# Sums of output-projection weights placed at other stages, weight loads on another queue, and two block products interleaved by token tile

## The chip, the cores and the metric

The program runs on one core of one Trainium2 chip. The core has five engines, which work at the same time and meet through semaphores: TensorE (PE: matrix products and transposes), VectorE (DVE), ScalarE (ACT), GpSimd (POOL) and SyncE (SP), which here only issues transfers. ACT and POOL can issue transfers too. Each engine, and each engine's line of transfers, works its instructions off in order. The metric is the device time of one execution in microseconds (us), lower being better.

## The reference, cut to what matters

The model is a trunk of two decoder layers over 1024 positions of width 1024, everything in float32. Layer 0 has latent attention, layer 1 sliding-window attention; in both, four cross-attention heads over 256 memory rows run beside them, and all heads go through one output projection `w_o`, followed by a squared-ReLU MLP.

```python
for i in range(DEPTH):
    hn = rmsnorm(x, attn_norm_g[i])
    mix, q_cross = mla_mixer(...) if i % 2 == 0 else swa_mixer(...)
    cross = memory_cross_attention(q_cross, mem_n, w_mem_kv[i])
    x = x + jnp.concatenate([mix, cross], axis=-1) @ w_o[i]
    x = x + squared_relu_mlp(rmsnorm(x, mlp_norm_g[i]), mlp_w_up[i], mlp_w_down[i])
return rmsnorm(x, final_norm_g)
```

## The kernel before

**Precision.** PE multiplies in a reduced float32 form, so every operand is split into a high and a low part (`split`, L94: ACT copies the high part, L99; DVE subtracts to get the low part, L100), and a product takes three PE instructions (high x high, high x low, low x high).

**Order.** The source gives a program order. When the kernel is built, a planner simulates the engines with its own costs and fixes each engine's order: an instruction goes when its inputs are ready, earlier program order first. So an instruction can stand on its engine well ahead of its place in the source, and on the chip the fixed order is kept even if another instruction would be ready. A tile whose memory overlaps an older tile waits until that one has been used for the last time.

**The output projection** is a Strassen-like scheme with seven block products (`wo_phase`, from L1203): the 1024 x 1024 product is cut in halves by token, by feature and by column, and `steps` lists the products in the order 1, 5, 6, 3, 2, 7, 4, four steps (k-tiles) each, 28 in all. Each step is 12 PE instructions: four token tiles j, three products each. `prep` splits the activation block of a step and loads its weights, `mm(n, j)` does step n for token tile j, `add(p, j)` adds the finished bank to the running result, `stat` stores it and forms half a sum of squares, `norm(t)` finishes the norm of tile t, `xT_(t)` transposes the normed tile for the MLP. Products 6, 7 and 4 accumulate in the same four PSUM banks Y as product 1. Steps 20 to 23 are product 7, steps 24 to 27 product 4. Before, steps 0 to 23 each run all four token tiles; product 4 then runs tile by tile. Tiles 0 to 3 are finished by product 2, tiles 4 to 7 by products 7 and 4.

**The weight sums** that this scheme needs are made beforehand by `wo_sums`. For each of 8 units (n = 0 to 7; k-tile n // 2, column quarter n % 2) it loads four blocks of 128 x 256 of `w_o` (L585, or L590 for layer 1, where a block is two half loads), makes four DVE subtractions (L619 to L622), splits each of the four results (high part to a buffer of `his`, low part in place) and stores both parts to scratch memory `wt`, eight stores of 128 KB a unit (L611), all on SP's line. It is a generator: the code around it calls `next(summing)` where a piece is to go. `sets` are the load buffers, `his` the buffers of the high parts; a buffer is used again only when its store is done.

- Layer 0: one set and four `his`, in spare quarters of the tile f1. Two `next` calls stand ahead of each of the nine later turns of the loop over token tiles in the input projection (L667 to L681): one unit a tile. A turn transposes tile k (`a_T`), projects tile k - 1 (`a_in`) and transposes the compressed tile k - 2 (`a_cT`). After it come the values (`values_of`) together with cross-attention (`cross`: score products, a maximum on DVE, exponentials on ACT, a scaling on POOL, transposes, value products), and then the keys and queries of the heads, with head buffers in the pool `hb`.
- Layer 1: two sets of four quarters of f1 and three `his` (the tile wos in the pool wosp). The projection runs ten jobs (L2073: values, keys, then six of queries, numbers 4 to 9), each of two token halves with 24 products (`feat_mm`, L109 to L111). `in_w` (L1942) loads one job's raw weights (512 KB, L1947, one of two buffers "raw"), POOL scales them (L1951) and `split` makes wf, one of two pairs. The load of job n + 1 is asked for at the start of job n. From job 4 on, two `next` calls stand ahead of each half. A positions tile, posb, takes one of the two raw buffers at job 4, and POOL makes the eight distance tiles from it (L2024 to L2028). The queries q1 are twelve tiles of 128 x 1024; q1[10] and q1[11] are written by job 9.

## Time and profile before

| what | us |
|---|---|
| median of three runs | 2142.35 (2137.09 to 2142.85) |
| profiled execution, timed | 2142.25 |
| its span, first to last instruction | 2140.5 |
| mean granted clock of PE | 0.994 |
| input projection of layer 0, first to last product | 47.5 to 144.6 |
| output projection of layer 0, products 7 and 4 | 509.1 to 535.9 |
| query jobs 4 to 9 of layer 1, first to last product | 1263.2 to 1350.3 |
| output projection of layer 1, start of product 7 | 1474.8 |

How to read the rows quoted below. In a timeline: start in us, duration, engine, line of the source, operation, written tile <- read tiles, shapes, count of merged instructions, and in brackets the idle time before it with what ended it. In a table of waits: who waited, for whom, us in total, times, longest. In a table of windows: the stretch, its length, then for PE, PE's weight loads, DVE, ACT and POOL the busy us and the instructions, then PE's granted clock, the mean busy share of the 16 transfer engines, and GB/s. In a table of lines: line, engine, operation, tiles, shapes and count, then busy us, mean ns of one, and the idle time before them with what ended it. A PE instruction's duration overlaps the next one's, so the pace is read from start to start. "SPq" is SP's line of transfers.

### The profile page before, as it was taken

Reading aid. Unit: us, or ns where it says so; the run is one execution under the profiler, and the core shown is the slowest. Engines: PE = TensorE matmul, PEld = TensorE weight load, DVE = VectorE, ACT = ScalarE, POOL = GpSimd, SP = SyncE. Lnnn points to the kernel's source line nnn. Section 1 sums busy time; section 2 is a strip of 40 time slices with the busy share of each in tenths; the row PEclk is TensorE's granted clock in tenths of the full one; section 3 lists DMA queues with packets and bytes.
Section 4 is the critical chain, followed back from the end, with each engine's and each line's share of the span. In section 5 each row is a group of like instructions: output and inputs, shape, how many; then the busy total and the mean of one; then the engine's idle time right before and its main releaser. Section 6 shows DMA issues by size and latency. Waiting matters only on the chain. (4 is left out here: it accounts for less than half of the span.)

```text
span 2140.5 us, 29718 instructions
## 1 busy us (share of the span) xinstructions
PE 2070.5 (97%) x9832; PEld 1690.8 (79%) x9832; DVE 1543.8 (72%) x3011; ACT 1150.0 (54%) x2504; POOL 161.9 (8%) x224
## 2 busy tenths in 40 slices
PE   7999999999899999999999997999999999999998
PEld 6888778777687878888888876778778778888886
DVE  7675688876976776976557466897987766976565
ACT  5555477767654444444445553877654443444452
POOL 0013100001000000000011331531000000000000
PEclk9999999999999999999999998999999999999999
DMA  8532225266244446944432236147254446955342
GB/s 270 175 102 71 49 63 131 55 202 211 94 157 162 149 140 227 322 147 152 142 119 90 66 93 192 41 132 247 89 168 162 138 133 220 327 162 154 117 119 89
DMA packets 209796, 314.43 MB, mean 147 GB/s; under 512 B 21629, under 2 KB 101994, under 8 KB 209642
## 3 DMA queue, kind: packets, MB, share of 16 engines
q1 hardware_dynamic: 203200, 296.77, 43.6%
q0 software_dynamic: 4016, 13.12, 1.7%
q10 hardware_dynamic: 2426, 2.65, 0.4%
q8 instruction: 77, 1.26, 0.3%
q14 instruction: 77, 0.63, 0.1%
HBM read 206.34 MB, written 93.63 MB: 140 GB/s over the span
## 5 line engine op out<-in xcount | busy, mean ns | idle before, releaser
L1403 ACT ACTIVATE mr<-mr,gcol 128x256 f32<-128x256 f32 (+1 forms) x160 | 67.8, 478 | 80.2 <-DMA mr<-in_mlp_w_up_dram 73.0
L1403 ACT ACTIVATE d<-d,gcol 128x256 f32<-128x256 f32 x128 | 57.5, 500 | 89.1 <-DMA d<-in_mlp_w_up_dram 81.6
L1844 PE MATMUL psy<-g 128*128 128x512 f32 x256 | 99.9, 390 | 0.0
L1845 PE MATMUL psy<-g 128*128 128x512 f32 x256 | 99.6, 389 | 0.0
L1846 PE MATMUL psy<-g 128*128 128x512 f32 x256 | 99.3, 389 | 0.0
L99 ACT ACTIVATE g<-i 128x512 fp32r<-128x512 f32 x79 | 49.6, 628 | 87.8 <-PE psz L1845 45.0
L100 DVE TENSOR_TENSOR g<-i,g 128x512 fp32r<-128x512 f32 x79 | 55.5, 702 | 48.5 <-ACT g L99 48.3
L99 ACT ACTIVATE uh<-i 128x512 fp32r<-128x512 f32 x66 | 41.6, 630 | 86.3 <-PE psy L1845 40.7
L99 ACT ACTIVATE i<-mr 128x512 fp32r<-128x512 f32 x78 | 49.0, 628 | 71.1 <-PE psy L1845 20.7
L953 ACT ACTIVATE p<-pss 128x512 f32<-128x512 f32 x108 | 63.6, 593 | 42.5 <-PE pss L932 42.3
L100 DVE TENSOR_TENSOR pl<-p,ph 128x512 fp32r<-128x512 f32 (+1 forms) x96 | 61.7, 652 | 25.4 <-ACT ph L99 24.8
L807 DVE TENSOR_REDUCE m<-psx 128x1 f32<-128x128 f32 (+5 forms) x96 | 70.3, 749 | 11.3 <-PE psx L803 11.2
L100 DVE TENSOR_TENSOR uh<-i,uh 128x512 fp32r<-128x512 f32 x66 | 45.6, 690 | 45.1 <-ACT uh L99 44.8
L1844 PE MATMUL psz<-g 128*128 128x512 f32 x192 | 74.7, 389 | 0.0
L1845 PE MATMUL psz<-g 128*128 128x512 f32 x192 | 74.7, 389 | 0.0
L1846 PE MATMUL psz<-g 128*128 128x512 f32 x192 | 74.7, 389 | 0.0
L100 DVE TENSOR_TENSOR i<-mr,i 128x512 fp32r<-128x512 f32 x78 | 53.7, 688 | 22.5 <-ACT i L99 22.2
L1725 DVE TENSOR_TENSOR mqf<-mqq,mqf 128x512 f32<-128x512 f32 x64 | 43.1, 687 | 22.5 <-DMA mqq<-in_mlp_w_down_dram 22.3
L99 ACT ACTIVATE ph<-p 128x512 fp32r<-128x512 f32 (+1 forms) x96 | 56.4, 599 | 1.3
L1845 PEld LDWEIGHTS psy<-g 128*128 128x128 f32 x256 | 48.1, 188 | 9.9
L1846 PEld LDWEIGHTS psy<-g 128*128 128x128 f32 x256 | 48.0, 188 | 10.0
L1507 PE MATMUL psu<-g,i 128*128 128x512 f32 x120 | 49.3, 411 | 6.8 <-ACT d L1546 4.1
(703 smaller groups left out, 6975.9 us busy)
## 6 DMA issues: line engine op xcount, KB each, us to landing
i<-hd SPq DMA_DIRECT2D x154, 256.0 KB
hd<-uh SPq DMA_DIRECT2D x76, 256.0 KB
hd<-ul SPq DMA_DIRECT2D x76, 256.0 KB
mr<-in_mlp_w_up_dram SPq DMA_DIRECT2D x36, 512.0 KB
hd<-x SPq DMA_DIRECT2D x72, 256.0 KB
mr<-hd SPq DMA_DIRECT2D x70, 256.0 KB
d<-in_mlp_w_up_dram SPq DMA_DIRECT2D x32, 512.0 KB
mqq<-in_mlp_w_down_dram SPq DMA_DIRECT2D x32, 512.0 KB
```

Source lines behind the costliest of these rows:

```text
L99: r = nc.scalar.activation(hi, src, AF.Copy)
L100: nc.vector.tensor_tensor(lo, src, f32(hi), ALU.subtract)
L807: nc.vector.reduce_max(m8s[h][:, i : i + 1], ps[:, c], axis=AX, negate=True)
L953: nc.scalar.activation(p, ps, AF.Exp, scale=SC)
L1403: nc.scalar.activation(w[:, k, :], w[:, k, :], AF.Copy, scale=g_mlp[layer][:, k0 + k : k0 + k + 1])
L1507: nc.tensor.matmul(ps, wh[:, k, :], xh[:, k, :], start=p in (1, 2, 5) and k == 0, stop=False, skip_group_check=True)
L1725: G(self.b(a, k), self.b(c, k), self.b(a, k), SUB)
L1844: nc.tensor.matmul(ps, ah[:, j, :], bh, start=p in (1, 5, 2) and k == 0, stop=False, skip_group_check=True)
L1845: nc.tensor.matmul(ps, ah[:, j, :], bl, start=False, stop=False, skip_group_check=True)
L1846: nc.tensor.matmul(ps, al[:, j, :], bh, start=False, stop=k == NP - 1, skip_group_check=True)
```

## The change

It has four edits.

1. Layer 0's sums are cut in two. Units 0 to 3 stay in the input projection with one set, at half the pace: one `next` ahead of the transposes and one behind the projection, and with one set the generator has extra empty steps, so that a unit takes two tiles, with a step between load and subtractions and one between subtractions and splits. Units 4 to 7 go to the values loop, two `next` calls behind each of tiles 2 to 7, with four sets and eight `his` in a new tile of 24 KB a partition (pool wop). All four are loaded as soon as the tile may be written. The pool is released ahead of `hb`, whose buffers take its memory.
2. Layer 1's `his` become eight quarters of q1[10] and q1[11]; the pool wosp goes.
3. The raw weights of jobs 4 to 9 are loaded from ACT's line and not from SP's.
4. In `wo_phase`, in both layers, the preparations of steps 24 to 27 and the norms of tiles 0 to 3 stand ahead of step 20. Products 7 and 4 then run tile by tile in the order 7.0, 7.1, 4.0, 7.2, 4.1, 7.3, 4.2, 4.3, each with its add, stat and (for 4) norm; `xT_` 0 to 5 follow the second to sixth and the last of these.

```diff
-    def wo_sums(layer, sets, his):
+    def wo_sums(layer, ns, sets, his):
...
-        V, ct, ns = nc.vector.tensor_tensor, [0], len(sets)
+        V, ct, step = nc.vector.tensor_tensor, [0], len(sets)
...
         def run():
-            for n in range(ns):
+            for n in ns[:step]:
                 load(n)
             yield
-            for n in range(8):
+            if step == 1:
+                yield
+            for n in ns:
...
                 V(s[3], s[3], s[2], ALU.subtract)
+                if step == 1:
+                    yield
                 put(n, 0)
                 put(n, 1)
                 yield
                 put(n, 2)
                 put(n, 3)
-                if n + ns < 8:
-                    load(n + ns)
+                if n + step in ns:
+                    load(n + step)
                 yield
+                if step == 1:
+                    yield
...
-    summing = wo_sums(0, [quarters[0:4]], quarters[4:8])
+    summing = wo_sums(0, range(4), [quarters[0:4]], quarters[4:8])
...
-        for _ in range(2 if k else 0):
+        if k:
             next(summing, None)
...
             a_in(k - 1)
+        if k:
+            next(summing, None)
...
+    wop = pool("wop")
+    wos = wop.tile([P, 24, 256], F32, name="wos")
+    wos = [wos[:, i, :] for i in range(24)]
+    summing = wo_sums(0, range(4, 8), [wos[i : i + 4] for i in range(0, 16, 4)], wos[16:])
+    next(summing)
...
         values_of(t)
+        for _ in range(2 if t > 1 else 0):
+            next(summing, None)
...
+    wop.release()
     hb = pool("hb")
...
-        for n in range(N - 4):
+        for n in range(N - 8):
...
+        for n in range(nprep, N):
+            prep(n)
+        for i in range(2):
+            q = m.quad(f"q{i}", F32R)
+            X[i + 1] = [q[:, 0:4, :], q[:, 4:8, :]]
         for j in range(4):
-            for n in range(N - 4, N):
+            norm(j)
+        for i, (p, j) in enumerate(((7, 0), (7, 1), (4, 0), (7, 2), (4, 1), (7, 3), (4, 2), (4, 3))):
+            for n in range(20 if p == 7 else 24, 24 if p == 7 else 28):
                 mm(n, j)
-            add(4, j)
-            stat(4 + j, 0)
-            norm(4 + j)
-            if j:
-                xT_(2 + j)
+            add(p, j)
+            stat(4 + j, int(p == 7))
+            if p == 4:
+                norm(4 + j)
+            t = {1: 0, 2: 1, 3: 2, 4: 3, 5: 4, 7: 5}.get(i)
+            if t is not None:
+                xT_(t)
...
-            nc.sync.dma_start(out=raw, in_=wsv[:, :, c0 : c0 + P])
+            (nc.scalar if wf is not None else nc.sync).dma_start(out=raw, in_=wsv[:, :, c0 : c0 + P])
...
-                wosp = pool("wosp")
-                wos = wosp.tile([P, 3, 256], F32, name="wos")
-                summing = wo_sums(1, [quarters[0:4], quarters[4:8]], [wos[:, e, :] for e in range(3)])
+                wos = [f32(q1[10 + i_ // 4][:, (i_ % 4) * 256 : (i_ % 4) * 256 + 256]) for i_ in range(8)]
+                summing = wo_sums(1, range(8), [quarters[0:4], quarters[4:8]], wos)
...
-    wosp.release()
```

More of the change, by code (lines that the diff above doesn't have):

```diff
@@ L590, in w_rows @@
             nc.sync.dma_start(out=dst[g * 64 : g * 64 + 64], in_=w_o[layer, h * 64 : h * 64 + 64, cols])
-    wts = {}
-    def wo_sums(layer, sets, his):
-        ds = wts[layer] = {p: [dram.tile([P, 4, 512], F32, name=f"wt{layer}_{p}{e}") for e in "hl"] for p in (5, 7, 6, 4)}
-        V, ct, ns = nc.vector.tensor_tensor, [0], len(sets)
+    wts = [{p: [dram.tile([P, 4, 512], F32, name=f"wt{layer}_{p}{e}") for e in "hl"] for p in (5, 7, 6, 4)} for layer in range(2)]
+    def wo_sums(layer, ns, sets, his):
+        V, ct, step = nc.vector.tensor_tensor, [0], len(sets)
         def load(n):
@@ L601, in load @@
             for i, (kt, e) in enumerate(((k, 0), (k, 1), (k + 4, 1), (k + 4, 0))):
-                w_rows(layer, kt, slice(e * 512 + c * 256, e * 512 + c * 256 + 256), sets[n % ns][i])
+                w_rows(layer, kt, slice(e * 512 + c * 256, e * 512 + c * 256 + 256), sets[n % step][i])
         def put(n, i):
             k, c = divmod(n, 2)
-            s = sets[n % ns][i]
+            s = sets[n % step][i]
             hi, lo = his[ct[0] % len(his)].bitcast(F32R), s.bitcast(F32R)
@@ L609, in put @@
             split(s, hi, lo)
-            for d_, t_ in zip(ds[(5, 7, 6, 4)[i]], (hi, lo)):
+            for d_, t_ in zip(wts[layer][(5, 7, 6, 4)[i]], (hi, lo)):
                 nc.sync.dma_start(out=d_[:, k, c * 256 : c * 256 + 256], in_=f32(t_))
         def run():
-            for n in range(ns):
+            for n in ns[:step]:
                 load(n)
             yield
-            for n in range(8):
-                s = sets[n % ns]
+            if step == 1:
+                yield
+            for n in ns:
+                s = sets[n % step]
                 V(s[0], s[1], s[0], ALU.subtract)
@@ L1367, in wo_phase @@
                 m.fill.append(fills[n // 14]())
-            if n == 20:
-                for i in range(2):
-                    q = m.quad(f"q{i}", F32R)
-                    X[i + 1] = [q[:, 0:4, :], q[:, 4:8, :]]
             for j in range(4):
```

7 lines of the change are left out of this document (removed).

## The prediction

> **What bounds the kernel now.** I read the page first, then PE's waits and windows in each of the stages that the diff touches, and last the timelines of the engines there.
>
> ```profile
> PE 2070.5 (97%) x9832; PEld 1690.8 (79%) x9832; DVE 1543.8 (72%) x3011; ACT 1150.0 (54%) x2504; POOL 161.9 (8%) x224
> PEclk9999999999999999999999998999999999999999
> ```
>
> PE is busy for 97% of the span, so time is to be had only where PE stands still or runs slowly. One slice of the 40 has a lower granted clock, about 1284 to 1337 us. That is layer 1's query projection, where the second edit lies. PE's waits from 1263 to 1352 have one row, and the windows show the stretch and the one before it:
>
> ```profile
> PE psf L109 <- ACT wf L99: 13.8, 3, 6.9
> core 0: us, PE busy (x) PEld busy (x) DVE busy (x) ACT busy (x) POOL busy (x), PEclk, DMA share, GB/s
> 1263.00:1290.00 27.00, 27.00 (x121) 22.36 (x120) 18.22 (x33) 12.28 (x25) 12.14 (x30) 1.00 0.48 152
> 1290.00:1340.00 50.00, 36.16 (x153) 29.23 (x152) 31.25 (x68) 20.80 (x50) 7.95 (x9) 0.86 0.59 182
> ```
>
> All of PE's 13.8 us of waiting is for split weights (wf), three times. The timelines of POOL, ACT, PE and SP say why:
>
> ```profile
> 1274.89 0.49 POOL L2028 TENSOR_SCALAR_AFFINE_SELECT df<-df 128x128 f32<-128x128 f32 x1
> 1277.66 1.22 DVE L100 TENSOR_TENSOR wf<-wsr,wf 128x1024 fp32r<-128x1024 f32 x1
> 1294.72 0.40 SPq L611 DMA_DIRECT2D wt_7l<-fb  x1
> 1295.23 0.38 SPq L1947 DMA_DIRECT2D wsr<-in_swa_w_in_dram  x1
> 1299.91 1.90 POOL L1951 TENSOR_TENSOR wsr<-wsr,gcol 128x1024 f32<-128x1024 f32 x1 [24.53 <-DMA wsr<-in_swa_w_in_dram]
> 1301.84 1.06 ACT L99 ACTIVATE wf<-wsr 128x1024 fp32r<-128x1024 f32 x1 [1.19 <-POOL wsr L1951]
> 1302.95 0.80 PE L109 MATMUL psf<-xnh,wf 128*128 128x512 f32 x1 [6.92 <-ACT wf L99]
> 1313.60 0.42 SPq L1947 DMA_DIRECT2D wsr<-in_swa_w_in_dram  x1
> 1327.76 0.39 SPq L1947 DMA_DIRECT2D wsr<-in_swa_w_in_dram  x1
> ```
>
> Job 7's raw weights go into the buffer of posb, which POOL has finished with when its last distance tile ends at 1275.4; they are issued at 1295.2, after stores of the weight sums (L611) on the same queue. So the load stands some 20 us behind other traffic in SP's line; POOL idles 24.5 us for it, ACT follows, PE comes last. Job 8's buffer is free at 1278.9, when DVE's split of job 6 ends, and its load is issued at 1313.6.
>
> What holds SP is seen in the waits of SP and of ACT:
>
> ```profile
> SPq L611 <- ACT wos L99: 21.1, 7, 16.3
> ACT wos L99 <- DMA wt_6h<-wos: 6.7, 5, 2.2
> ACT wos L99 <- DMA wt_5h<-wos: 6.6, 3, 3.8
> 1253.08 0.42 DVE L406 COPY fb<-psco 128x256 f32<-128x256 f32 x1
> 1263.00 0.39 PE L111 MATMUL psf<-xnh,wsl 128*128 128x512 f32 x1
> 1264.64 1.03 ACT L99 ACTIVATE wos<-fb 128x256 fp32r<-128x256 f32 x3
> ```
>
> SP waits 16.3 us in one piece for the first split of a sum. That split starts right after job 3's last product, since the three buffers wos lie where job 3's split weights lay. (The row at 1253.08 is the last of the cross-attention, for later.) Afterwards the splits wait 13.3 us for a store to give one of the three buffers back.
>
> **The change, part by part.**
>
> *Layer 1's loads and sums.* The loads of jobs 4 to 9 go from SP's line to ACT's; the sums' high parts go to eight quarters of q1[10] and q1[11]. One job is 48 products:
>
> ```profile
> 1263.23 0.39 PE L109 MATMUL psf<-xnh,wf 128*128 128x512 f32 x1
> 1274.11 0.39 PE L109 MATMUL psf<-xnh,wf 128*128 128x512 f32 x1
> 1350.05 0.39 PE L111 MATMUL psf<-xnh,wf 128*128 128x512 f32 x1
> ```
>
> 10.88 us a job, 0.227 us a product. Six jobs need 65.3 us; they take 87.0 (1263.2 to 1350.3). Of the 21.7 between, 13.8 are the waits. Part of the rest is score products that stand there in both kernels, part is slow clock: 1290 to 1340 lacks at most 14% of 50 us, 7 us, some of it while PE idled anyway; I take 3.5. So the edit can give 0 to 17.3 us.
>
> What is late next? From issue to DVE's split the chain is 4.7 (1295.23 to 1299.91), then 1.9, 1.06 and 1.22, some 9 us, less than a job. Job 7's load, issued by 1276, is split by 1286 and needed at 1296; job 8's is split when job 6 gives its wf buffer back at 1296 and needed at 1307; job 9's likewise 11 us later. The load adds a wait to ACT, whose line is in order: behind it stand the evictions of q, and behind those PE, which has four banks, 5.44 us each. The wait must therefore outlast some 16 us to be felt. Six issues at 0.4 us are hidden in ACT's idle (29.2 of 50 us).
>
> The sums stay slow. Of the eight rows of stores, the first and the last by time:
>
> ```profile
> L611 SPq DMA_DIRECT2D wt_5h<-wos x8: 344/382/535, 1265.1 to 1325.8; - x8
> L611 SPq DMA_DIRECT2D wt_4l<-fb x8: 319/400/448, 1270.0 to 1331.9; - x8
> ```
>
> Eight units in 67 us, 8.4 us each, since a unit's loads follow the stores of the unit two before. But they start earlier. q1 lies over the cross-attention's buffers and job 2's split weights, free at about 1253 (its last eviction) rather than 1263. Eleven us of start, and fewer waits for buffers, put the last store from 1332 to about 1318 (my estimate). Job 9's evictions into q1[10] and q1[11], the new wait, come at about 1323. Yet ACT's and DVE's orders are fixed at build time, and a split of wf behind a late sum is late with it; for that I leave 2.3 us. **15 us less**, ends 0 and 17.3, nearest to the waits' row.
>
> *Layer 0's sums.* Lines of 100 to 146 by shape, waits of PE from 48 to 146, and the windows:
>
> ```profile
> L619 DVE TENSOR_TENSOR fa<-fa 128x256 f32<-128x256 f32 x4 | 1.7, 426 | 10.7 <-DMA fa<-in_w_o_dram 10.7
> L100 DVE TENSOR_TENSOR fa<-fa 128x256 fp32r<-128x256 f32 x16 | 6.0, 419 | 0.0
> PE psct L573 <- DVE qc L340: 1.6, 2, 1.0
> PE psct L574 <- POOL fa L304: 1.4, 2, 0.9
> PE psT_a L208 <- DVE xhls L100: 1.3, 3, 0.7
> 146.00:190.00 44.00, 41.78 (x293) 36.22 (x294) 29.06 (x62) 30.45 (x103) 17.39 (x12) 1.00 0.08 21
> ```
>
> In four units DVE stands 10.7 us for w_o, and PE loses 4.3 us to DVE's lateness (rope's POOL included). With a unit every second tile and a step between load and subtraction most of this goes: 3 us less, ends 0 and 4.3. The other four units go to the values stage: 8 DVE instructions each at 0.42 make 13.4 us, against 14.9 us of DVE idle in 146 to 190; 16 ACT splits (three took 1.03 us above) make 5.5 against 13.5. DMA share there is 0.08, so SP's 16 loads and 32 stores find a free line, but they can start only when the input weights' memory is free. In sum it fits, in order it will not quite: behind a subtraction stand softmax maxima, behind those PE. I take 2.5 us more, ends 0 and 13.4 (nothing hidden). Head 0's buffers now wait for the last of these stores; no product of this stage reads them, so I take nothing for it. **0.5 us less.**
>
> *The last two block products.* The instructions are the same ones in another order. DVE's adds, SP's last load of product 4's operands and PE's first use of them, and the windows of each layer:
>
> ```profile
> L1291 DVE TENSOR_TENSOR d<-pswy,d 128x512 f32<-128x512 f32 x4 | 2.7, 686 | 0.4 <-PE pswy L1287 0.3
> 1471.53 0.32 SPq L1261 DMA_DIRECT2D mqf<-wt_4l  x1
> 1488.83 0.48 PE L1285 MATMUL pswy<-mqf,g 128*128 128x512 f32 x1
> 500.00:530.00 30.00, 29.86 (x145) 24.20 (x145) 18.48 (x50) 22.81 (x56) 5.17 (x11) 1.00 0.51 185
> 530.00:570.00 40.00, 35.66 (x169) 27.69 (x167) 38.97 (x79) 31.10 (x66) 1.44 (x3) 1.00 0.13 47
> 1460.00:1495.00 35.00, 34.64 (x168) 28.58 (x167) 21.14 (x51) 27.76 (x67) 7.08 (x13) 1.00 0.69 245
> 1495.00:1535.00 40.00, 36.21 (x163) 28.21 (x163) 38.84 (x81) 30.18 (x65) 1.62 (x3) 0.96 0.13 46
> ```
>
> After the products DVE is full (39.0 and 38.8 of 40 us) and PE loses 4.3 and 3.8 us; before it DVE has 11.5 and 13.9 us free. A tile's product is 12 x 0.227 = 2.7 us. Tile 4's last product becomes third of eight instead of fifth, 5.4 us sooner; tile 5's fifth instead of sixth, 2.7 us sooner; tiles 6 and 7 stay. So one or two tiles' work (four DVE subtractions at 0.69 and a norm) may move into the free time, if ACT, also near full, brings their transposes. New waits: product 4 of a tile now waits for add 7 in the same bank, 0.69 us under the 2.7 of the product between; and its operands, the last issued at 1471.5 and first used at 1488.8, are needed 5.4 us sooner, with 11.9 to spare. I take 1.5 us a layer, **3 us less**, ends 8.1 less (all of both losses) and 4 more (an add late behind DVE's line in every second turn).
>
> *Sum.* The profiled execution took 2142.25 us, span 2140.5 and 1.75 around it; the three runs have the median 2142.35, so no correction. 2142.25 - 15 - 0.5 - 3 = 2123.75: **2124 us**.
>
> A page of the Trainium skill speaks against the first term: "DMA: Bandwidth & Descriptors", section "Issuing engines are not separate DMA queues", has it that issuing from several engines saves only the sequencer's time to start a transfer, usually small beside the transfer.
>
> **The rivals.**
>
> *Transfers, not SP's line, hold the loads.* Then the move saves three issues at 0.4, 1.2 us, and the time is 2137.6. Against it: the transfer engines are 59% busy there, job 7's load landed 4.7 us after issue, and the 20 us lie before it. 0.07. The rule above would make this of the change.
>
> *The sums' own pace binds.* ACT and DVE, in order, wait for a unit every 8.4 us, where program order has one in 5.44. Over eight units that is 23.7 us of lag. A split may be late by the 10.9 us of a job less its own 2.3, so 8.6 are covered, and the earlier start takes off 11 in full (4 us of stall, within the forecast) or half of it: then 9.6 us of stall stay, 7.7 are gained, 2131. For it: the stores wait mostly for ACT's splits, ACT's splits for stores. 0.20.
>
> *Values and products lose.* DVE's line delays the softmax by 6 us more than I took: 2130. 0.10. *They gain:* DVE's free time takes two tiles in each layer, 6 us: 2118. 0.07.
>
> *Slower: ACT's line.* The load of the next job stands on ACT behind splits that wait for their sums, and each of jobs 5 to 9 starts its 9 us chain when ACT comes to it. It decides where ACT reaches a load more than 2 us (10.88 less 9) into the job before. If ACT comes 7.5 us late, each of the five jobs stalls 5.5 us, 27.5 in all against 17.3 now: 2142.25 + 10.2 - 3.5 = 2149. Against it: the load depends on nothing of the sums, and its buffer is free early. 0.05.
>
> **How the numbers follow.** Forecast 0.51, with its own range 2118 to 2130. Range 2114 to 2137: it takes in the pace rival, both cases of values and products, and their bounds, and leaves out the transfer rival, the slower one and the tails. 0.3% is 6.4 us, about what a measurement can tell from no change: faster means under 2135.9. Forecast, pace, loss and gain make 0.88, less 0.02 of tails: 0.86; same 0.08; slower 0.06.
>
> **What would show it.** PE's waits for wf near 0 and clock 1.00 from 1263 on; loads wsr issued by ACT before 1280; POOL's 24.5 us gone; six jobs in under 72 us. First wos split near 1253. No 10 us of DVE waiting for w_o in the input projection; softmax chain ending within 3 us of now, measured from the first score product. After the products DVE still full, PE losing about 2.5 us a layer. Wrong would be: PE waiting for wf behind an ACT that waits for stores or w_o, or for q's banks.

## The result, and the profile after

| | median of 10 runs, us | profiled execution: time, span, us |
|---|---|---|
| before | 2142.22 (2137.09 to 2146.69) | 2142.25, 2140.5 |
| after | 2135.57 (2131.81 to 2137.80) | 2133.98, 2131.8 |

The ratio is 0.9970, with a 95% interval from 0.9958 to 0.9982: 6.4 us faster (3.9 to 9.0), where 18.5 were forecast. The time lies inside the stated range of 2114 to 2137 us, near its upper end, and outside the narrower range, 2118 to 2130, that the forecast itself was given.

The gain is small because layer 1 gives back part of what it gains, and layer 0's split gives back more than it gains. The table gives first and last starts of a stage's products in the two profiled executions.

| stage | before | after | gain |
|---|---|---|---|
| input projection, first to last product | 47.5 to 144.6 | 47.8 to 140.6 | 4.3 |
| last compressed-tile transpose to last key product (values, cross-attention, keys) | 155.2 to 206.1 | 151.2 to 208.8 | -6.7 |
| from there to the first block product | 206.1 to 450.4 | 208.8 to 454.3 | -1.2 |
| layer 0's block products, to the first product of the second half of the MLP | 450.4 to 859.0 | 454.3 to 861.1 | 1.8 |
| layer 1, first query product to last score product | 1263.2 to 1411.1 | 1265.6 to 1408.1 | 5.4 |
| layer 1's block products, to the same product of the MLP | 1413.9 to 1826.2 | 1410.9 to 1818.3 | 4.9 |

A single profile carries noise of its own: the input projection of seven profiled kernels in which it is untouched took 94.5 to 97.1 us, mean 95.9; in eleven that have the changed one it took 92.3 to 93.4, mean 93.0. So its gain is 2.9 us, and a row of the table is good to a microsecond or so.

**Layer 1.** PE's longest waits from 1240 to 1420 us, after:

```profile
PE psw L2062 <- DVE fb L2067: 8.9, 1, 8.9
PE psf L111 <- DVE wf L100: 1.5, 1, 1.5
```

The windows, with the columns explained ahead of the change, after:

```profile
1263.00:1290.00 27.00, 27.00 (x121) 22.36 (x120) 17.70 (x28) 12.32 (x25) 13.92 (x31) 1.00 0.50 147
1290.00:1340.00 50.00, 39.60 (x173) 32.40 (x172) 34.94 (x79) 22.88 (x55) 7.13 (x9) 0.90 0.58 184
1333.00:1338.00 5.00, 5.00 (x15) 4.23 (x16) 2.04 (x15) 2.83 (x14) 2.67 (x4) 0.51 0.00 0
```

The 13.8 us of waiting for wf are 1.5. In their place stands one wait of 8.9 us, of a score product (psw), and behind it 5 us at a granted clock of 0.51, another 2.4 us. Who is late is read from the timelines of ACT, POOL, DVE and PE:

```profile
1275.93 0.37 ACTq L1960 DMA_DIRECT2D wsr<-in_swa_w_in_dram  x1
1327.78 0.27 POOL L2058 COPY fb<-sinks_b 128x3 f32<-128x3 f32 x1 [22.57 <-DMA wt_6h<-q]
1331.15 0.35 DVE L2067 CUSTOM_DVE_ANT_0 fb<-psw,df,sinks_b 128x128 f32<-128x128 f32 x1
1332.93 0.47 PE L2062 MATMUL psw<-kh,q 128*128 128x128 f32 x1 [8.89 <-DVE fb L2067]
1334.27 0.73 PE L109 MATMUL psf<-xnh,wf 128*128 128x512 f32 x1
```

Job 7's load is issued at 1275.9 and no longer at 1295.2. But the last job's code also makes the scores of query block 0 (`s_qk(0, g)`), and their probabilities and sums (p, st) lie in f1[:, 0:2], the same memory as the two sets of the weight sums' load buffers. So POOL's first copy into it waited 22.6 us for a store of the sums, to 1327.8, and DVE, which in its order still had splits of the sums and evictions of the queries ahead, read the first score bank (L2067) only at 1331.2. Two score banks had been full since 1323; the third group of score products waited on PE, and the last job's products (psf), which need nothing of it, were queued behind. In time, the 8.9 us divide like this: 4.0 from the end of the last product (1324.0) to the end of POOL's copy (1328.0), 3.1 more until DVE's order reaches the bank, and 1.8 until PE goes on. This is a reading of the rows; what the wait would be without one of the parts it does not say.

The sums are as slow as before. SP's longest wait from 1263 to 1352, after:

```profile
SPq L610 <- ACT q L99: 26.1, 10, 23.1
```

Two of the eight rows of stores by tile (ns at least, median, at most; first and last start), after:

```profile
L610 SPq DMA_DIRECT2D wt_5h<-q x8: 328/382/530, 1267.5 to 1328.0; - x8
L610 SPq DMA_DIRECT2D wt_4l<-fb x8: 382/400/403, 1271.0 to 1331.5; - x8
```

And one unit of SP's timeline, after:

```profile
1316.54 0.38 SPq L610 DMA_DIRECT2D wt_5h<-q  x1
...
1319.99 0.40 SPq L610 DMA_DIRECT2D wt_4l<-fb  x1
1320.48 2.39 SPq L590 DMA_DIRECT2D fb<-in_w_o_dram  x4
1322.96 1.02 SPq L585 DMA_DIRECT2D fb<-in_w_o_dram  x2
1324.07 0.38 SPq L610 DMA_DIRECT2D wt_5h<-q  x1
```

The first store is at 1267.5, after a wait of 23.1 us for ACT's first split, which stands in ACT's order behind the evictions of job 3; the last is issued at 1331.5 (1331.9 before). The seven steps from the first to the eighth wt_5h take 60.5 us, 8.6 each on average; the first step takes 13.5 and the last, which has no loads in it, 3.9. In the unit shown, which takes 7.5, SP has no gap: eight stores 3.9 us, six loads 3.6.

**Layer 0.** The windows of the first part of the values stage, before and then after:

```profile
146.00:180.00 34.00, 31.93 (x224) 28.79 (x224) 23.40 (x52) 25.46 (x88) 15.00 (x11) 1.00 0.05 16
```

```profile
146.00:180.00 34.00, 26.84 (x184) 23.74 (x184) 32.33 (x69) 26.51 (x87) 11.44 (x8) 0.95 0.49 157
180.00:215.00 35.00, 34.73 (x195) 28.69 (x195) 19.81 (x41) 17.75 (x46) 8.93 (x9) 1.00 0.38 103
```

PE is busy 5.1 us less of the 34 where DVE goes from 23.4 to 32.3; the clock of 0.95 is another 1.7, and together that is the stage's loss. From 180 on PE loses next to nothing. The sums' 32 DVE instructions in that window took 16.5 us and not the 13.4 that the prediction took for them: the four subtractions of a unit 0.42 to 0.75 each. Its waits from 150 to 215, after:

```profile
PE pscT L388 <- POOL cps L428: 3.2, 2, 2.1
PE pscx L376 <- ACT cps L425: 1.6, 1, 1.6
PE psco L403 <- DVE cpT L392: 1.5, 1, 1.5
```

The first softmax group in the timelines of ACT, POOL and PE, before and then after:

```profile
152.83 0.48 ACT L425 ACTIVATE cps<-pscx,cst 128x256 f32<-128x256 f32 x1
156.70 1.89 POOL L428 TENSOR_TENSOR cps<-cps,cst 128x1024 f32<-128x1024 f32 x1 [3.68 <-issue]
```

```profile
148.84 0.47 ACT L425 ACTIVATE cps<-pscx,cst 128x256 f32<-128x256 f32 x1
150.86 1.59 ACT L99 ACTIVATE wos<-wos 128x256 fp32r<-128x256 f32 x4
152.36 0.46 ACT L425 ACTIVATE cps<-pscx,cst 128x256 f32<-128x256 f32 x1
154.33 1.90 POOL L428 TENSOR_TENSOR cps<-cps,cst 128x1024 f32<-128x1024 f32 x1 [7.19 <-DVE cst L426]
156.28 1.09 PE L388 MATMUL pscT<-ident,cps 128*128 128x128 f32 x8 [1.16 <-POOL cps L428]
```

Four splits of the sums (wos) stand on ACT between the first exponential of the group and the other three; POOL's scaling starts 5.5 us after that first exponential, where it was 3.9 before, and PE's transposes stand behind it.

**The block products.** The windows behind them, in both layers, after:

```profile
530.00:570.00 40.00, 37.36 (x182) 29.46 (x181) 39.05 (x78) 31.80 (x67) 2.17 (x4) 1.00 0.15 53
1495.00:1535.00 40.00, 36.74 (x166) 28.10 (x165) 39.39 (x75) 28.66 (x60) 1.08 (x2) 1.00 0.17 55
```

DVE is still full; PE loses 2.6 and 3.3 us where it lost 4.3 and 3.8, and the clock in the second is 1.00 where it was 0.96. Layer 0's stage lies some 4 us later than before; in a window that starts behind its last product PE loses 3.0. From the first block product to the MLP's second half, the four profiled kernels without edit 4 take 408.1 us in layer 0 and 411.2 in layer 1 on average, the sixteen with it 405.8 and 407.7: 2.3 and 3.5 less. So part of layer 1's 4.9 in the table is the single profile's noise.

### The profile page after: what moved, and what is told of

Its sections match the earlier page's. It is cut to its first block, busy times and chain, and to the rows that moved or that the text cites. A ratio compares the mean times of both kernels' runs of the same rounds, so it can differ in the third digit from the quotient of the medians.

```text
span 2131.8 us, 29731 instructions
## 1 busy us (share of the span) xinstructions
PE 2069.8 (97%) x9832; PEld 1691.2 (79%) x9832; DVE 1547.4 (73%) x3011; ACT 1149.5 (54%) x2504; POOL 163.6 (8%) x224
## 4 chain that ended last, share of the span: by engine, by line
PE 67%; DMA 11%; DVE 11%; ACT 5%; issue 3%; SPq 1%; POOL 1%; DVEq 0%; ACTq 0%; POOLq 0%
PE psy L1857 5%; PE psy L1859 5%; PE psy L1858 5%; PE psz L1858 4%; PE psz L1859 4%; PE psz L1857 4%; DMA mr<-in_mlp_w_up_dram 4%; PE pss L947 4%; PE pso L989 4%; DMA d<-in_mlp_w_up_dram 3%; PE psu L1520 3%; PE psu L1522 2%; PE psu L1521 2%; PE psv L1522 1%; PE psv L1521 1%
## 5 line engine op out<-in xcount | busy, mean ns | idle before, releaser
L821 DVE TENSOR_REDUCE m<-psx 128x1 f32<-128x128 f32 (+5 forms) x96 | 70.3, 749 | 11.3 <-PE psx L817 11.1
L1859 PEld LDWEIGHTS psy<-g 128*128 128x128 f32 x256 | 48.1, 188 | 10.0
L1857 PEld LDWEIGHTS psy<-g 128*128 128x128 f32 x256 | 48.1, 188 | 9.9
L1858 PEld LDWEIGHTS psy<-g 128*128 128x128 f32 x256 | 48.1, 188 | 9.9
```

Of the source, the lines that this page charges most:

```text
L821: nc.vector.reduce_max(m8s[h][:, i : i + 1], ps[:, c], axis=AX, negate=True)
L1857: nc.tensor.matmul(ps, ah[:, j, :], bh, start=p in (1, 5, 2) and k == 0, stop=False, skip_group_check=True)
L1858: nc.tensor.matmul(ps, ah[:, j, :], bl, start=False, stop=False, skip_group_check=True)
L1859: nc.tensor.matmul(ps, al[:, j, :], bh, start=False, stop=k == NP - 1, skip_group_check=True)
```

## The experiments

All ratios are to before, measured beside it; 0.001 is 2.1 us.

### The parts one by one

Each kernel is before with a part of the change: layer 0's sums (edit 1), layer 1's loads and high-part buffers (edits 2 and 3), these loads (edit 3), the order in `wo_phase` (edit 4), and all but layer 0's sums (edits 2 to 4). The core of edits 2 and 3 is:

```diff
-                wosp = pool("wosp")
-                wos = wosp.tile([P, 3, 256], F32, name="wos")
+                wos = [f32(q1[10 + i_ // 4][:, (i_ % 4) * 256 : (i_ % 4) * 256 + 256]) for i_ in range(8)]
...
-            nc.sync.dma_start(out=raw, in_=wsv[:, :, c0 : c0 + P])
+            (nc.scalar if wf is not None else nc.sync).dma_start(out=raw, in_=wsv[:, :, c0 : c0 + P])
```

> Before with layer 0's split of the weight sums alone (edit 1). Theory A (read from the two traces: the input projection gains 4.0 us, the values stage gives back 6.7 and the keys and heads 1.2): 3.9 us slower than before, last values-stage products about 3 us later, ratio 1.002. Rival (the sizes of the recorded forecast: 3 gained, 2.5 given back): 0.5 us faster, ratio 0.9998.

> Before with edits 2 and 3 alone (layer 1: eight high-part buffers in q1[10] and q1[11], wf loads on ACT's line). Theory A: the sums still take SP some 8.4 us a unit and end near 1331, so the first score products, whose buffers are those of the sums, stand about 9 us; 5 us faster, ratio 0.9977. Rival (the recorded forecast): 15 us faster, ratio 0.993.

> Before with the last two block products alternating by token tile alone (edit 4). Theory A (the milestones of the two traces: 1.8 us in layer 0, 4.9 in layer 1): 6.7 us faster, ratio 0.9969. Rival (the recorded forecast): 3 us faster, ratio 0.9986.

> Before with the loads of jobs 4 to 9 on ACT's line alone (edit 3; three high-part buffers stay). Theory A: PE's 13.8 us of waiting for wf go, but the first score products stand for the sums' buffers, which end no earlier than 1332: gain between 0 and 5 us, and less than or the same as with edit 2 beside it. Rival 1 (the wf waits were all there was): 11 to 14 us faster. Rival 2 (transfers, not the line, hold the loads): 1.2 us faster and wf waits stay near 13 us.

> The changed kernel with layer 0's sums left as they were before (edits 2, 3 and 4 alone). Theory A (the parts add up, and layer 0's split is a loss of some 4 to 6 us): 12 us faster than before, 5 to 6 faster than the changed kernel, ratio to before 0.9943. Rival (the recorded forecast, layer 0's split a gain of 0.5): as the changed kernel or slower, ratio 0.997.

| kernel | median, us | ratio (95%) |
|---|---|---|
| layer 0's sums only | 2146.18 | 1.0027 (1.0018 to 1.0037) |
| layer 1's loads and sums only | 2133.77 | 0.9967 (0.9957 to 0.9978) |
| layer 1's loads only | 2136.98 | 0.9985 (0.9974 to 0.9995) |
| block products only | 2135.72 | 0.9976 (0.9964 to 0.9987) |
| all but layer 0's sums | 2129.22 | 0.9953 (0.9941 to 0.9965) |

Layer 0's split costs 5.8 us, layer 1's edits gain 7.1, the products 5.1. The sum, 6.4, is the change's own gain: the parts add up. Without layer 0's part 10.1 us are gained, somewhat less than the 12.2 of the two others together, within the intervals. The products' 5.1 lies between the 6.7 read from the two traces and the 3 of the recorded forecast. With the loads alone the new wait stands already; PE's waits from 1260 to 1350 in that kernel (its lines are those of before):

```profile
PE psw L2049 <- DVE fb L2054: 8.3, 1, 8.3
PE psf L111 <- DVE wf L100: 2.5, 1, 2.5
```

Its last stores by tile:

```profile
L611 SPq DMA_DIRECT2D wt_4l<-fb x8: 319/338/407, 1268.5 to 1329.5; - x8
```

So the line of issues did hold the loads: the wf waits go with it. The eight high-part buffers make the sums little quicker: from the first store to the last they take 66.0 us with three buffers (1263.5 to 1329.5) and 63.0 with edits 2 and 3 together (1263.1 to 1326.1). Beside the loads these buffers are worth 3.9 us by the two ratios, whose intervals overlap. The 3.2 us that the loads alone gain (1.1 to 5.6) do not speak against the rule of the Trainium skill that the prediction cites, by which it made 1.2 us of the move; the rows do: 11 us of PE's waits for wf went, and others took their place.

### Layer 1: the place of block 0's scores

```diff
-            if n + 1 == len(jobs):
-                for g in (range(3), (3,))[i]:
-                    s_qk(0, g)
...
             sink(j, i, feat_mm(w, i, str(n + 2)))
+            if n + 1 == len(jobs) and i:
+                for g in range(4):
+                    s_qk(0, g)
+                    if g:
+                        s_norm(0, g - 1)
```

> The changed kernel with the scores of query block 0 behind the last query job's products and not ahead of them; the sums stay slow. Theory A (the score products stand for the sums' buffers, with the last job's products queued behind them on PE): the 8.9 us wait goes, the clock stays 1.00, and PE loses 3 to 5 us instead for the softmax of block 0 that nothing covers now; 4 to 6 us faster than the changed kernel, ratio to before 0.9945. Rival (the place costs as much as the wait): within 1 us of the changed kernel, ratio 0.997.

> Layer 0's sums as before, layer 1's edits and the product order as changed, block 0's scores behind the last query job. Theory A (the two losses are apart from each other): 12.2 us of the run without layer 0's split and some 6 of the later scores add up, 18 us faster than before, about 2121, ratio 0.9915. Rival (they overlap): no better than the better of the two, 2126, ratio 0.994.

| kernel | median, us | ratio (95%) |
|---|---|---|
| changed, scores behind job 9 | 2126.50 | 0.9939 (0.9927 to 0.9951) |
| the same without layer 0's split | 2120.66 | 0.9909 (0.9896 to 0.9922) |

Four lines moved give 6.6 us more than the change (0.9970 to 0.9939), and 9.4 us where layer 0 is left alone (0.9953 to 0.9909). In the first of them PE's longest wait from 1240 to 1420 is:

```profile
PE psw L2062 <- DVE fb L2067: 3.2, 1, 3.2
```

and PE's timeline has, at the end of the last query job:

```profile
1332.76 0.39 PE L111 MATMUL psf<-xnh,wf 128*128 128x512 f32 x1
1332.98 0.22 PE L2062 MATMUL psw<-kh,q 128*128 128x128 f32 x1
```

The six jobs take 67 us (1265.7 to 1332.8) where they took 87 before and 82 after; some 4 us of the 87 and of the 82 were score products, which stood between the jobs and now follow them. The sums end no earlier (last store issued at 1330.7), so the gain is that of the place: no query product stands behind the late bank any more. Theory A holds for the wait and the time (0.9939 for 0.9945), not for the clock: it is 1.00 up to 1333, but 0.50 from 1337 to 1342, behind the 3.2 us that stay. With the later place the edits of layer 1 are worth 7.1 + 6.6 to 9.4, 14 to 16 us. What the later place alone would give the kernel before was not run; there PE waits 0.9 us for DVE's reading of the scores.

### Layer 1: what sets the pace of the sums

The stores of layer 1's high parts from ACT's line:

```diff
-            for d_, t_ in zip(wts[layer][(5, 7, 6, 4)[i]], (hi, lo)):
-                nc.sync.dma_start(
+            for q_, d_, t_ in zip((nc.scalar if layer else nc.sync, nc.sync), wts[layer][(5, 7, 6, 4)[i]], (hi, lo)):
+                q_.dma_start(
```

A block's two half loads made one, in `w_rows`, for the sums alone:

```diff
-        for g in range(2):
-            h = 3 * (2 * a + g) + e
-            nc.sync.dma_start(out=dst[g * 64 : g * 64 + 64], in_=w_o[layer, h * 64 : h * 64 + 64, cols])
+            src = w_o[layer, 0:768].rearrange("(a g e r) c -> a e g r c", a=2, g=2, e=3)[a, e]
+            nc.sync.dma_start(out=dst, in_=src[:, :, cols])
```

A third set, in free memory and that of the second buffer of the tile di in `dist_tile`:

```diff
-                summing = wo_sums(1, range(8), [quarters[0:4], quarters[4:8]], wos)
+                summing = wo_sums(1, range(8), [quarters[0:4], quarters[4:8], [third[:, i_, :] for i_ in range(4)]], wos)
```

> The changed kernel with layer 1's stores of the sums' high parts issued from ACT's line, right behind the split that makes them; low parts and loads stay on SP. Theory A1 (the pace of a unit is SP's line: some 15 issues a unit): the last store of the sums comes 10 us earlier or more, at 1320, the wait of the score products goes from 8.9 to under 2 us, 8 to 11 us faster than the changed kernel, ratio to before 0.992. Rival A2 (the pace is the round trip of store, load, sum and split of a set, not the number of issues): last store within 3 us of 1331, wait over 6 us, 0 to 3 us faster, ratio 0.996.

> Both of the above together. Theory A1: the wait is gone already by the stores on ACT, so the later place only uncovers the softmax: 2 to 4 us slower than the stores on ACT alone, ratio 0.9935. Rival A2: as the later place alone, ratio 0.9945.

> The changed kernel with the two half loads of a weight block of layer 1's sums made one load of the same bytes: 4 loads a unit instead of 6 to 8, so 12 issues a unit instead of 14 to 16. Theory A1 (SP's issues set the pace of 8.2 us a unit: eight stores 4.0, six loads 3.4 to 4): a unit every 7 us, last store near 1323 rather than 1331, the score products' wait from 8.9 to under 2 us, 6 to 9 us faster than the changed kernel, ratio 0.9935. Rival A2 (the round trip of a set binds at the same pace): last store within 3 us of 1331, 0 to 2 us faster, ratio 0.9965.

> Layer 0's sums as before, scores behind the last job, merged loads. If A1 holds for the merged loads, the last 3 us of wait at the scores go too: 2 to 4 us faster than without the merging, 2118, ratio 0.990. By A2 the same as without the merging, ratio 0.9915.

> The changed kernel with a third set of load buffers for layer 1's sums; all issues stay on SP. Theory A1 (SP's issues set the pace): still 8.2 us a unit, last store within 3 us of 1331, ratio 0.997. Rival A2 (the round trip of two sets does): a unit every 6 to 7 us, last store near 1320, the score products' wait under 2 us, ratio 0.993.

> The changed kernel with the third set and with the high parts stored from ACT's line. Theory A1 alone or A2 alone would have shown in the single runs; if both bind at about the same pace, only this run is quicker: a unit every 6 us, last store near 1318, the score products' wait under 2 us, ratio 0.993. Rival A3 (something else, DVE's and ACT's fixed orders, sets the pace): last store near 1328, ratio 0.998.

The pace is a seventh of the time from the first to the eighth store wt_5h.

| kernel | ratio (95%) | pace of a unit, us | last store issued |
|---|---|---|---|
| changed | 0.9970 (0.9958 to 0.9982) | 8.6 | 1331.5 |
| high parts from ACT | 0.9981 (0.9970 to 0.9992) | 8.1 | 1329.2 |
| three sets | 0.9964 (0.9952 to 0.9976) | 7.9 | 1331.9 |
| three sets, high parts from ACT | 0.9980 (0.9969 to 0.9991) | 7.1 | 1319.9 |
| high parts from ACT, scores behind | 0.9959 (0.9947 to 0.9971) | 7.7 | 1327.3 |
| merged loads | 1.0133 (1.0119 to 1.0147) | 11.3 | 1363.9 |
| layer 0 as before, scores behind, merged loads | 1.0086 (1.0070 to 1.0101) | 11.3 | 1354.9 |

SP's issues and the round trip of two sets bind at nearly the same pace: one relieved leaves 8.1 or 7.9 us, both 7.1. Only with both do the stores end 12 us earlier. And yet that kernel is not faster than the change. PE's longest waits from 1240 to 1420 in it:

```profile
PE psw L2062 <- DVE fb L2067: 3.9, 1, 3.9
PE psf L111 <- DVE wf L100: 2.7, 2, 1.5
PE psf L109 <- ACT wf L99: 2.4, 1, 2.4
```

The timelines of POOL, ACT, DVE and PE in it, ahead of the first reading of a score bank:

```profile
1313.57 0.19 POOL L2058 COPY fb<-sinks_b 128x3 f32<-128x3 f32 x1 [3.20 <-DMA wt_7l<-fb]
1316.33 0.44 ACTq L1960 DMA_DIRECT2D wsr<-in_swa_w_in_dram  x1
1325.40 1.23 DVE L100 TENSOR_TENSOR wf<-wsr,wf 128x1024 fp32r<-128x1024 f32 x1 [5.65 <-ACT wf L99]
1328.97 0.40 PE L111 MATMUL psf<-xnh,wf 128*128 128x512 f32 x1
1330.08 1.41 DVE L340 SCALAR_TENSOR_TENSOR q<-psf,q 64x512 fp32r<-64x512 f32 x2 [0.66 <-ACT q L339]
1331.52 0.35 DVE L2067 CUSTOM_DVE_ANT_0 fb<-psw,df,sinks_b 128x128 f32<-128x128 f32 x1
```

First, POOL's copy comes at 1313.6 and not at 1327.8, and yet the first bank is read no sooner: at 1331.5, against 1331.2 in the changed kernel. On DVE the reading (L2067) stands behind the split of the last job's weights and the evictions of the query jobs (L340), which take turns with ACT's (L339). The wait is 3.9 us and not 8.9 because PE comes to it some 5 us later: its last product ahead of the wait starts at 1329.0, in the changed kernel at 1323.7. So DVE's line is a cause of its own beside the sums; what share of the 8.9 us each has is not shown. The prediction saw neither. Second, PE is that late because it waits 5.1 us for wf. ACT now issues half of the sums' stores, and its loads stand among them: those of the last two jobs are issued at 1301.7 and 1316.3, in the changed kernel at 1285.7 and 1298.1. So loads stand behind stores again, now in ACT's line and no longer in SP's; that this alone makes wf late is read from the rows and was not tested. With the scores behind the last job, too, the stores on ACT are a loss: 0.9959 against 0.9939, 4.3 us, which neither theory had. Expectation A1 fails for the stores on ACT (0.9981 and no 0.992); A2 fails for the third set.

The merged loads are a miss of another kind: a load of the same 128 KB as one instruction lands much later. The loads of the first two blocks of a unit and the subtraction that waits for them, merged:

```profile
1316.02 1.09 SPq L590 DMA_DIRECT2D fb<-in_w_o_dram  x2
...
1324.55 0.43 DVE L624 TENSOR_TENSOR fb<-fb 128x256 f32<-128x256 f32 x1 [5.69 <-DMA fb<-in_w_o_dram]
```

and in the changed kernel, with four half loads, whose issue at 1320.48 is shown above:

```profile
1324.76 0.42 DVE L620 TENSOR_TENSOR fb<-fb 128x256 f32<-128x256 f32 x1 [0.80 <-DMA fb<-in_w_o_dram]
```

7.4 us from the last issue's end to the subtraction, against 1.9. The number of issues was no test of SP's line with such a landing, and the run says nothing on A1.

### Layer 0: what the values stage pays for

All calls for units 4 to 7 behind the cross-attention:

```diff
-        for _ in range(2 if t > 1 else 0):
-            next(summing, None)
     for _ in crossing:
         pass
+    for _ in summing:
+        pass
```

The same with one set:

```diff
-    summing = wo_sums(0, range(4, 8), [wos[i : i + 4] for i in range(0, 16, 4)], wos[16:])
+    summing = wo_sums(0, range(4, 8), [wos[0:4]], wos[16:])
```

The subtractions of units 4 to 7 on POOL:

```diff
-        V, ct, step = nc.vector.tensor_tensor, [0], len(sets)
+        V, ct, step = (nc.vector if layer or ns[0] == 0 else nc.gpsimd).tensor_tensor, [0], len(sets)
```

Six units in the projection and two in the values, and all eight in the projection; in the first a third `next` stands behind `a_cT`, in the second one more behind `a_T`, and the values have none:

```diff
-    summing = wo_sums(0, range(4), [quarters[0:4]], quarters[4:8])
+    summing = wo_sums(0, range(6), [quarters[0:4]], quarters[4:8])
...
-    summing = wo_sums(0, range(4, 8), [wos[i : i + 4] for i in range(0, 16, 4)], wos[16:])
+    summing = wo_sums(0, range(6, 8), [wos[i : i + 4] for i in range(0, 8, 4)], wos[16:])
...
-    summing = wo_sums(0, range(4), [quarters[0:4]], quarters[4:8])
+    summing = wo_sums(0, range(8), [quarters[0:4]], quarters[4:8])
```

All five have block 0's scores behind job 9; 0.9939 (0.9927 to 0.9951) is what they are compared with.

> The changed kernel with block 0's scores behind the last job, and with layer 0's units 4 to 7 asked for behind the whole cross-attention, so that an instruction of the softmax goes first where both are ready. Theory A (the values stage loses its 6.7 us because DVE and ACT, in a fixed order, do the sums ahead of the softmax): the values stage loses 2 us or less, 4 to 5 us faster than with the scores behind alone, 2122, ratio 0.992. Rival (the sums' work itself does not fit, or the memory of the head buffers comes free too late): the loss stays, only later, in the keys and heads; ratio 0.994.

> The changed kernel with block 0's scores behind the last job, and the sixteen subtractions of layer 0's units 4 to 7 on POOL and not on DVE; the splits stay. Theory A (DVE has no room: 23.4 of the 34 us from 146 to 180 were busy before, and the sums bring 13.4): 6.7 us of DVE work go, DVE falls to about 27 of 34, the values stage loses 2 us or less, 4 to 5 us faster than with the scores behind alone, ratio to before 0.992. Rival B (order or memory costs it): the loss stays near 6.7, ratio 0.994. Rival C (POOL's scaling of the softmax stands behind the sums): more loss, PE waiting for POOL, ratio 0.996.

> The changed kernel with block 0's scores behind the last job and layer 0's units 4 to 7 behind the cross-attention, with one set of load buffers and not four, so that a unit starts only when the stores of the one before have landed. Theory A: the same DVE work is spread over some 50 us and not 34, so the values stage loses 3 to 4 us and not 6.7, ratio 0.993. Rival B: the loss stays at 6.7 or grows, as the head buffers wait for the last store, ratio 0.9945.

> The changed kernel with block 0's scores behind the last job, with six units of layer 0's sums in the input projection (three steps of the generator a tile) and two in the values stage. Theory A (the amount of sums' work in the values stage sets the loss): the stage loses some 3 us and not 6.7, the input projection still gains 3, 3 us faster than with the scores behind alone, ratio to before 0.9925. Rival (a fixed cost, such as the order of the softmax's instructions around any sums): the loss stays at 6, ratio 0.994.

> The changed kernel with block 0's scores behind the last job, with all eight units of layer 0's sums in the input projection in four steps a tile, so that a step lies between a load and its subtractions, and none in the values stage. Theory A: the values stage is as before, the input projection gains 1 to 3 us on before since DVE meets loads that have landed; 1 to 3 us faster than with layer 0's sums as before and the scores behind, 2119, ratio 0.990. Rival (eight units load the projection too much, however spaced): as with layer 0's sums as before, ratio 0.991.

| layer 0's units 4 to 7 | median, us | ratio (95%) | projection, us | values stage, us |
|---|---|---|---|---|
| in the values loop (compared with) | 2126.50 | 0.9939 (0.9927 to 0.9951) | 93.1 | 57.7 |
| behind the cross-attention | 2130.01 | 0.9947 (0.9934 to 0.9959) | 92.6 | 57.6 |
| subtractions on POOL | 2129.12 | 0.9938 (0.9927 to 0.9950) | 93.3 | 59.1 |
| one set | 2130.05 | 0.9951 (0.9939 to 0.9962) | 93.1 | 58.3 |
| two of the four in the projection | 2123.25 | 0.9917 (0.9902 to 0.9931) | 93.9 | 55.9 |
| all four in the projection, spaced | 2120.85 | 0.9902 (0.9886 to 0.9919) | 93.9 | 50.9 |

The values stage took 50.9 us before. In the first three theory A fails: neither a later call, nor one set, nor the subtractions on POOL takes the loss away. With the later calls DVE is busy for 32.3 of the 34 us from 146 to 180, as in the changed kernel. That fits the planner, which puts the sums where an engine is free in its plan, whatever their place in the source. Moving the subtractions to POOL did not even relieve DVE. Its window there, with the columns as above:

```profile
146.00:180.00 34.00, 27.20 (x178) 24.74 (x176) 31.67 (x58) 24.30 (x81) 22.36 (x23) 0.95 0.54 173
```

Its group of splits in that window, by line and shape (count, busy us, mean ns), and then the same group in the changed kernel:

```profile
L100 DVE TENSOR_TENSOR wos<-wos 128x256 fp32r<-128x256 f32 x16 | 15.1, 977 | 0.3 <-ACT wos L99 0.2
```

```profile
L100 DVE TENSOR_TENSOR wos<-wos 128x256 fp32r<-128x256 f32 x16 | 7.0, 467 | 0.0
```

The sixteen splits took 0.98 us each instead of 0.47. With two units in the values stage the window is:

```profile
146.00:180.00 34.00, 28.38 (x194) 25.37 (x193) 26.06 (x56) 25.49 (x87) 13.62 (x10) 0.95 0.22 71
```

and PE's waits from 150 to 215 in it are:

```profile
PE pscT L388 <- POOL cps L428: 3.2, 2, 2.1
PE pscx L376 <- ACT cps L425: 1.6, 1, 1.6
```

DVE has 8 us free there, and the stage still loses 5.0 of its 6.7 to 6.8 us, by the same two waits as with four units: half the work leaves three quarters of it, between theory A's 3 and the rival's 6. So room on DVE over the window was not what was missing. With no unit there the loss is gone. That it hangs on the first units, whose instructions stand between those of the first softmax groups on ACT and DVE, is read from the timeline above and not shown by a run: which of these instructions would have to move was not tried.

The last row has the lowest ratio of all: 2120.85 us, 21 us less than before and 14.6 less than the change by the two ratios. In it the input projection holds all eight units and still has two thirds of the changed one's gain (93.9 against 93.0; 95.9 before), with a step between a load and its subtractions: DVE waits 9.2 us for `w_o` from 40 to 146, where it waited 17.1 before. It can't be told apart from the version with layer 0 as before (0.9909).

## Why the prediction was right and wrong

The forecast gain was 18.5 us and the measured one 6.4. Of the 12.1 between, 7.9 are layer 1's term and 6.3 layer 0's; the products gave 2.1 more than forecast.

**Layer 1's loads and sums: forecast 15, measured 7.1 alone.** This is the step that failed most. Its first half held: the 20 us stood in SP's line, the load is issued by 1276, the 9 us chain is hidden, PE waits 1.5 us for wf. "What is late next?" was answered from the loads alone. The text named job 9's evictions into q1[10] and q1[11] as the new wait and did not ask who else writes where the sums lie. Block 0's scores write over the sums' load sets, ahead of the last job's products on PE, and behind the query evictions on DVE. The wait of 8.9 us and 2.4 of slow clock behind it make 11.3, and 17.3, the upper end, less 11.3 is 6.0, near the 7.1. With the scores moved, 14 to 16 are there: the wait that the term was to remove was read rightly, and the failed step is the answer to what is late next, which left 2.3 us for all of it where 8.9 us at a score bank and 2.4 of slow clock stood.

**The early start of the sums** did not come: the first split was expected near 1253 and came at 1267.1. Free memory was taken for the start; ACT's order, with the evictions of job 3 ahead, set it. Already before, the split at 1264.64 followed on ACT without a gap on such an eviction (L333, 1264.03 to 1264.62), so the row that the prediction read as a wait for memory did not show one. With it fell the last store at 1318.

**The pace rival** (0.20, 2131) was right that the sums' pace binds, and is the nearest of the cases in kind. It looked for the stall at the splits of wf, where 1.5 us stand. Nearest in time is the transfer rival's 2137.6, by luck: its mechanism is out.

**Layer 0's sums: forecast 0.5 less, measured 5.8 more.** The projection's term was right, 2.9 for 3. The values' term was mis-sized: 6.7 for 2.5, with 1.2 more up to the block products, a stretch for which the prediction took nothing; the cause of the 1.2 was not looked for. It weighed the work against DVE's idle time in the 44 us from 146 to 190. The run with two units shows that the sum of idle time was the wrong measure: 5.0 us of the loss are there with DVE at 26 of 34 us. "In order it will not quite" fit, the text said; the order, as far as the timeline shows it, costs more than the room that it counted. The rival in which the values lose 6 us more was right in kind, and near in size with 4.2 and the 1.2.

**The block products: forecast 3 less, measured 5.1** (2.8 to 7.7), inside the ends of 8.1 less and 4 more. Both directions of the reasoning hold: DVE stays full behind the products, and PE loses less. Part of the difference was not weighed: layer 1's clock behind the products went from 0.96 to 1.00, 1.6 us of 40 at most. That the sum came nearer by it is luck.

**The other rivals.** The transfer rival is out, as the waits for wf went with the move of the issues. The rival of ACT's line did not show in the change; a part of it shows in the runs that put the stores on ACT too, 5.1 us of waits for wf.

**The signs.** Right: wf waits near 0 (1.5), job 7's load on ACT before 1280 (those of jobs 8 and 9 came at 1285.7 and 1298.1), POOL's long wait for a load down (10.5 us at most, from 24.5), DVE's waits for `w_o` down (7.5 us from 40 to 146, from 17.1), DVE full behind the products with PE losing 2.6 and 3.3 for 2.5. Wrong: a clock of 1.00 throughout (0.90 from 1290 to 1340), six jobs under 72 us (82), first split near 1253 (1267.1), softmax within 3 us (6.7).

## What to carry to other kernels

When a wait goes, follow the slow producer and not only the wait: list everyone who writes or reads the memory that it holds, and what stands behind each of them on an in-order engine. Idle time of an engine, summed over a window, is no room for work that lands between the links of a chain; ask what the chain's next instruction would stand behind. A product that may be late goes behind those that can't be.

## What the hardware showed that was not expected

- **One load in two row groups lands late.** 128 KB as one instruction over two groups of 64 rows: 7.4 us from issue to use, against 1.9 as two instructions. The Trainium skill, "DMA: Bandwidth & Descriptors", section "Why a DMA increments its semaphore by 16 and not by 1", has it that the number of transfer engines is the largest one up to 16 that divides the size of the slowest dimension on both sides; on the side of `w_o` the kernel makes that 2 here. The delay agrees; the number of engines is not seen in a row of this case.
- **POOL beside DVE.** DVE's 128 x 256 subtraction of a split took 0.98 us, the mean of sixteen, where POOL ran subtractions in the same window, 0.47 in the changed kernel. The Trainium skill, "SBUF — State Buffer", section "Who interferes with whom", says that a DVE instruction with two inputs in SBUF contends with a POOL instruction that reads SBUF. The rows agree, and work moved from DVE to POOL saved DVE 0.7 us of 32.3.
- **A stall costs twice.** After the wait of 8.9 us PE ran 5 us at a clock of 0.51. With the scores behind the last job it waited 3.2 us, and ran at 0.50 from 1337 to 1342 all the same: the shorter wait had a slow stretch as long.
